# One level of Strassen's algorithm for the two products of a channel mixer

## The chip, the cores and the metric

The kernel runs on one core of one Trainium2 chip. The metric is the device time of one execution in microseconds (us). A core has a matrix engine (TensorE, here PE, with its weight loads as PEld), three others for elementwise work (VectorE or DVE, ScalarE or ACT, GpSimd or POOL) and a queue that issues transfers (SyncE or SP). Each works through its own list of instructions in order and waits on the others by semaphores. SBUF and PSUM are the on-chip memories: PE writes its products into banks of PSUM.

## The reference

One decoder layer over 1024 tokens of width 1024: two kinds of attention, merged and projected, and then the channel mixer with 4096 inner features, which is what the change touches:

```
x = x + rmsnorm(merged @ w_out, post_norm_mix)
h2 = rmsnorm(x, pre_norm_mlp)
y = square(relu(h2 @ w_up)) @ w_down
x = x + rmsnorm(y, post_norm_mlp)
```

All in float32.

## The kernel before

Every float32 matrix is held as a sum of two rounded parts, hi and lo (`hilo`, L80: a copy to hi on ACT, a subtraction for lo on DVE or another engine), and every product is made of three passes in `mm3` (L85): hi by hi, hi by lo, lo by hi. One pass over 128 rows and 512 columns is one matmul instruction, called a product or a pass below.

Ahead of the channel mixer, `mix_front` and `mix_back` (L914, L937) go over 8 tiles of 128 tokens: w_out, norm, residual, second norm, transposes on PE, and the split of the transposed activation into h2 (two halves of 512 tokens, each hi and lo, 8 blocks of 128 features).

The mixer follows in 16 groups of two chunks of 128 inner features. `up(g)` loads two chunks of w_up (512 KB each), splits them (`wchunk`, L132), makes 2 x 2 x 8 x 3 products into PSUM (`big`), and then relu and square on ACT and the split of the result (`uh`, `ul`) on DVE. It stays in SBUF. `down(g)` takes these as stationary operands with the two chunks of w_down (`dh`, `dl`), goes over 8 token tiles and two column halves, and adds each bank `D` to the sum `yac` in SBUF on DVE (L1040). In the program `up(g + 1)` stands before `down(g)`, and a scheduler orders each engine's list. Loads go through two buffers `raw`. The last group also makes the final norm, tile by tile, and stores the output. The last tile is cut into pieces of 512, 256 and 256 columns.

## Time and profile before

| | us |
|---|---|
| median of 3 runs (1430.97 to 1434.01) | 1433.59 |
| span of the profiled execution | 1434.7 |
| PE busy in it | 1403.1 (98%) |
| DVE busy | 764.5 (53%) |
| ACT busy | 534.0 (37%) |
| POOL busy | 231.8 (16%) |
| the channel mixer, from its first product to the end | 722.6 to 1434.7 |

The profile is one execution recorded by the hardware. A page sums it up (busy time by engine, the chain of instructions that ended last, groups of instructions, transfers), and views of the trace give the instructions of one engine in order of time, groups of equal instructions, and the busy time of each engine in a stretch. PEclk is the clock that PE was granted, as a share of full speed.

### The profile page before, as it was taken

The numbers are of one execution on the slowest core, as the hardware profiler recorded it, in microseconds if no ns is written. First come the engines' busy times: TensorE is split into PE (matmuls) and PEld (weight loads), VectorE is DVE, ScalarE is ACT, GpSimd is POOL, SyncE is SP. The second block draws the span as 40 slices with busy tenths as digits, with TensorE's granted clock in tenths as the row PEclk, the third lists the DMA queues.
The fourth block names the chain that finished last, engine by engine and source line by source line (L and its number), as shares of the span: only waits on it lengthen the run. The fifth ranks groups of instructions, "written<-read, shape, count | busy, mean of one in ns | idle before, by whom it ended". The sixth has DMA issues, their size and how long they took to land.

```text
span 1434.7 us, 17738 instructions
## 1 busy us (share of the span) xinstructions
PE 1403.1 (98%) x6650; PEld 1155.2 (81%) x6650; DVE 764.5 (53%) x1339; ACT 534.0 (37%) x977; POOL 231.8 (16%) x316
## 2 busy tenths in 40 slices
...
GB/s 316 118 93 127 112 120 92 124 113 87 100 98 93 130 176 245 220 228 89 94 98 88 59 31 43 45 59 60 56 31 32 59 59 59 30 45 44 59 1 205
DMA packets 64183, 141.24 MB, mean 98 GB/s; under 512 B 8417, under 2 KB 22625, under 8 KB 64097
## 3 DMA queue, kind: packets, MB, share of 16 engines
...
## 4 chain that ended last, share of the span: by engine, by line
PE 84%; DMA 6%; DVE 5%; ACT 2%; issue 2%; POOL 1%; SPq 1%; POOLq 0%; DVEq 0%; ACTq 0%
PE big L87 12%; PE big L88 12%; PE big L89 12%; PE D L88 8%; PE D L87 8%; PE D L89 8%; PE F L87 4%; PE F L88 4%; PE F L89 4%; DMA raw<-w_o 2%; PE T L784 2%; PE big L758 1%; PE big L755 1%; PE big L759 1%; DVE wlo L83 1%
## 5 line engine op out<-in xcount | busy, mean ns | idle before, releaser
L89 PE MATMUL big<-h,wlo 128*128 128x512 f32 x748 | 295.1, 395 | 7.5 <-DVE wlo L83 7.5
L87 PE MATMUL big<-h,whi 128*128 128x512 f32 x748 | 294.2, 395 | 1.5 <-DVE sg L907 0.8
L88 PE MATMUL big<-l,whi 128*128 128x512 f32 x748 | 294.4, 394 | 0.0
L82 ACT CAST whi<-raw 128x1024 fp32r<-128x1024 f32 (+1 forms) x89 | 91.8, 1033 | 441.0 <-PE big L88 382.6
L1040 DVE TENSOR_TENSOR yac<-D,yac 128x512 f32<-128x512 f32 (+1 forms) x225 | 154.0, 686 | 143.3 <-PE D L89 142.6
L88 PE MATMUL D<-dl,uh 128*128 128x512 f32 (+1 forms) x516 | 200.1, 388 | 0.0
L87 PE MATMUL D<-dh,uh 128*128 128x512 f32 (+1 forms) x516 | 200.0, 388 | 0.0
L89 PE MATMUL D<-dh,ul 128*128 128x512 f32 (+1 forms) x516 | 199.5, 387 | 0.0
L89 PEld LDWEIGHTS big<-h,wlo 128*128 128x128 f32 x748 | 141.1, 189 | 43.0 <-DVE wlo L83 12.1
L83 DVE TENSOR_TENSOR wlo<-raw,whi 128x1024 fp32r<-128x1024 f32 (+1 forms) x73 | 94.5, 1296 | 143.1 <-ACT whi L82 138.3
L87 PEld LDWEIGHTS big<-h,whi 128*128 128x128 f32 x748 | 140.9, 189 | 32.8 <-ACT h L82 1.2
L88 PEld LDWEIGHTS big<-l,whi 128*128 128x128 f32 x748 | 141.1, 189 | 30.9
L103 POOL TENSOR_SCALAR s<-s 128x1 f32<-128x1 f32 x24 | 4.9, 205 | 772.9 <-DVE s L1046 692.1
L87 PEld LDWEIGHTS D<-dh,uh 128*128 128x128 f32 x516 | 96.9, 188 | 20.2
L88 PEld LDWEIGHTS D<-dl,uh 128*128 128x128 f32 x516 | 96.9, 188 | 20.0
L89 PEld LDWEIGHTS D<-dh,ul 128*128 128x128 f32 x516 | 96.9, 188 | 19.9
L88 PE MATMUL F<-l,whi 128*128 128x512 f32 x260 | 103.4, 398 | 3.2 <-DVE l L83 3.2
L87 PE MATMUL F<-h,whi 128*128 128x512 f32 x260 | 104.7, 403 | 0.6 <-ACT h L82 0.5
L89 PE MATMUL F<-h,wlo 128*128 128x512 f32 x260 | 103.2, 397 | 0.0
L83 DVE TENSOR_TENSOR dl<-raw,dh 128x1024 fp32r<-128x1024 f32 x32 | 39.1, 1225 | 94.8 <-ACT dh L82 94.8
L82 ACT CAST dh<-raw 128x1024 fp32r<-128x1024 f32 x32 | 33.5, 1050 | 132.3 <-DMA raw<-w_down 111.1
L768 POOL TENSOR_SCALAR e<-e,bsm 128x128 f32<-128x128 f32 (+3 forms) x64 | 49.1, 771 | 138.3 <-DVE bsm L767 99.6
...
## 6 DMA issues: line engine op xcount, KB each, us to landing
raw<-w_in SPq DMA_DIRECT2D x42, 512.0 KB, 3.8
raw<-w_up SPq DMA_DIRECT2D x32, 512.0 KB, 3.8
raw<-w_down SPq DMA_DIRECT2D x32, 512.0 KB, 3.6
x<-x SPq DMA_DIRECT2D x24, 512.0 KB, 3.6
gate<-tmp SPq DMA_DIRECT2D x32, 256.0 KB, 2.0
sg<-gate SPq DMA_DIRECT2D x32, 256.0 KB, 4.0
raw<-w_o SPq DMA_DIRECT2D x15, 512.0 KB, 4.7
xT<-xT SPq DMA_DIRECT2D x16, 256.0 KB, 5.8
```

The lines of the kernel that those rows point to most:

```text
L82: nc.scalar.copy(out=hi, in_=src)
L83: (eng or nc.vector).tensor_tensor(out=lo, in0=src, in1=hi.bitcast(F32), op=ALU.subtract)
L87: nc.tensor.matmul(out, lhsT=lh, rhs=rh, start=first, stop=False)
L88: nc.tensor.matmul(out, lhsT=lh, rhs=rl, start=False, stop=False)
L89: nc.tensor.matmul(out, lhsT=ll, rhs=rh, start=False, stop=last)
L103: nc.gpsimd.tensor_scalar(out=out, in0=ss, scalar1=1.0 / dim, scalar2=EPS, op0=ALU.mult, op1=ALU.add)
L755: nc.tensor.matmul(o, lhsT=qh, rhs=kh[:, kc], start=True, stop=False)
L758: nc.tensor.matmul(o, lhsT=qh, rhs=kl[:, kc], start=False, stop=False)
L759: nc.tensor.matmul(o, lhsT=ql, rhs=kh[:, kc], start=False, stop=True)
L768: nc.gpsimd.tensor_scalar(out=e[:, :nk], in0=e[:, :nk], scalar1=sm[:, 3:4], scalar2=1.0, op0=ALU.mult, op1=ALU.mult)
L784: nc.tensor.transpose(pt[:, c0:c0 + P], es2[qi][:, kb * P:(kb + 1) * P], ident)
L1040: nc.vector.tensor_tensor(out=y[:, nn], in0=ps, in1=y[:, nn], op=ALU.add)
```

## The change

The mixer's two matrix products are each cut into 2 x 2 blocks, and the eight block products are replaced by seven, between sums of blocks (Winograd's form of Strassen's algorithm). There are now two stages with the result in DRAM between them.

- `mix_back` writes the transposed activation H unsplit (odd k on ACT, even k on DVE). `split_b1` splits the first half of the tokens during tile 4. The first w_up pair is loaded during the last tile, and its products p1 and p2 (banks `F` and `O`) stand around the last tile's transposes.
- After the last tile, a loop over k makes four sums of blocks of H (b11, b12, b22, b21 in place, two on DVE and two on POOL) and splits five operands `B1[p]` for p = 5, 6, 7, 4, 3, with the subtraction on DVE, for p = 7 on POOL.
- The up stage goes over 16 pairs j of w_up chunks. `up_w` makes four sums of the weights on POOL (`s`) and five splits (`oh`, `ol`, six buffers each); `raw1` and `raw2` share the two buffers `raw`. `up_head` and `up_tail` of neighbouring pairs are interleaved. Products accumulate in banks a, b and c, copies are kept on ACT (`snap`) and added on DVE (`summed`). Relu and square are on ACT. Four further sums on POOL combine the squared results for the next stage (`v`), and all seven parts go to DRAM (`UC`, 256 KB each).
- The down stage goes over 8 groups. `down_ops` loads four chunks of w_down (`r1`, `r2`) and the seven parts (`ur`, two buffers), makes four sums on POOL (`t1`, `t2`, b12 and `t2` again), and splits both operands, four of the fourteen subtractions on POOL and ten on DVE. `down_step` makes a product for one of four token tiles and adds the bank to `yac`, 28 such additions a group. One bank is carried on from one product to the next, and opened anew at products 1, 5 and 2.
- The cut of the last tile is gone, and the final multiplication by `gpo` is on POOL.

The core of the diff:

```diff
-                hi, lo = act_k(h2[ti // 4], 4 * a + k)
+                dst = H[ti // 4][:, 4 * a + k, c]
                 gk = g_mlp[:, 4 * a + k:4 * a + k + 1]
                 src = pt[:, k * P:(k + 1) * P]
-                nc.scalar.activation(out=hi[:, c], in_=src, func=AF.Copy, scale=gk)
-                nc.vector.scalar_tensor_tensor(out=lo[:, c], in0=src, scalar=gk, in1=hi.bitcast(F32)[:, c],
-                                               op0=ALU.mult, op1=ALU.subtract)
+                if k % 2:
+                    nc.scalar.activation(out=dst, in_=src, func=AF.Copy, scale=gk)
+                else:
+                    nc.vector.tensor_scalar(out=dst, in0=src, scalar1=gk, scalar2=None, op0=ALU.mult)
...
+    H = [tl(act["0"], [P, KD, 512], F32, tag, 1) for tag in "hl"]
+    UC = {p: [tc.dram_tile([P, 2, 512], F32, name=f"uc_{p}_{g}") for g in range(NGRP)] for p in range(1, 8)}
...
+    def up_w1(j):
+        raw = tl(wst, [P, 1024], F32, "raw", 2)
+        nc.sync.dma_start(out=raw, in_=t["w_up"][2 * j])
+        hi, lo = tl(wst, [P, 1024], F32R, "whi", 2), tl(wst, [P, 1024], F32R, "wlo", 2)
+        hilo(hi, lo, raw)
+        ws = {1: (hi[:, :512], lo[:, :512]), 2: (hi[:, 512:], lo[:, 512:])}
+        return raw, ws
...
+    def split_b1():
+        hi, lo = act_set("2")
+        for k in range(0, KD, 2):
+            hilo(hi[:, k:k + 2, :], lo[:, k:k + 2, :], H[0][:, k:k + 2, :])
+        B1[1] = hi[:, 0:4, :], lo[:, 0:4, :]
+        B1[2] = hi[:, 4:8, :], lo[:, 4:8, :]
...
+        if ti == NT - 1:
+            early_up = up_w1(0)
         if len(pend) > 1:
             mix_back(*pend.pop(0))
+        if ti == 4:
+            split_b1()
+    banks[0] = dict(a=fbank(), b=tl(pss, [P, 512], F32, "O", 1))
+    up_mm(banks[0]["a"], early_up[1][1], B1[1], True)
+    up_mm(banks[0]["b"], early_up[1][2], B1[2], True)
     mix_back(*pend.pop())
...
+    for k in range(4):
+        b11, b21, b12, b22 = H[0][:, k, :], H[0][:, 4 + k, :], H[1][:, k, :], H[1][:, 4 + k, :]
+        of = {p: (B1[p][0][:, k, :], B1[p][1][:, k, :]) for p in (5, 6, 7, 4, 3)}
+        nc.vector.tensor_tensor(out=b11, in0=b12, in1=b11, op=sub)
+        hilo_on(nc.vector, *of[5], b11)
+        nc.gpsimd.tensor_tensor(out=b12, in0=b22, in1=b12, op=sub)
+        hilo_on(nc.vector, *of[3], b22)
+        nc.vector.tensor_tensor(out=b22, in0=b22, in1=b11, op=sub)
+        hilo_on(nc.vector, *of[6], b22)
+        hilo_on(nc.gpsimd, *of[7], b12)
+        nc.gpsimd.tensor_tensor(out=b21, in0=b21, in1=b22, op=sub)
+        hilo_on(nc.vector, *of[4], b21)
...
+    def up_w(j):
+        raw1, ws = early_up if j == 0 else up_w1(j)
+        raw2 = tl(wst, [P, 1024], F32, "raw", 2)
+        nc.sync.dma_start(out=raw2, in_=t["w_up"][2 * j + 1])
+        a11, a12, a21, a22 = raw1[:, :512], raw1[:, 512:], raw2[:, :512], raw2[:, 512:]
+        s = {p: tl(uw, [P, 512], F32, "s", 4) for p in (5, 6, 7, 3)}
+        def split(p, x):
+            hi, lo = tl(uw, [P, 512], F32R, "oh", 6), tl(uw, [P, 512], F32R, "ol", 6)
+            hilo(hi, lo, x)
+            ws[p] = hi, lo
+        nc.gpsimd.tensor_tensor(out=s[5], in0=a21, in1=a22, op=add)
+        split(5, s[5])
+        nc.gpsimd.tensor_tensor(out=s[6], in0=s[5], in1=a11, op=sub)
+        split(6, s[6])
+        nc.gpsimd.tensor_tensor(out=s[7], in0=a11, in1=a21, op=sub)
+        split(7, s[7])
+        split(4, a22)
+        nc.gpsimd.tensor_tensor(out=s[3], in0=a12, in1=s[6], op=sub)
+        split(3, s[3])
+        return ws
+    def snap(ps):
+        x = slot(2)
+        nc.scalar.copy(out=x, in_=ps)
+        return x
+    def relu2(x, src):
+        nc.scalar.activation(out=x, in_=src, func=AF.Relu)
+        nc.scalar.activation(out=x, in_=x, func=AF.Square)
+    def store_u(j, p, x):
+        nc.sync.dma_start(out=UC[p][j // 2][:, j % 2, :], in_=x)
+    def summed(j, p, x, ps, s):
+        nc.vector.tensor_tensor(out=x, in0=ps, in1=s, op=add)
+        relu2(x, x)
+        store_u(j, p, x)
+    def up_head(j, w, after=None):
+        b = banks.setdefault(j, {})
+        if j:
+            b["a"] = tl(ps4, [P, 512], F32, "a", 2)
+            up_mm(b["a"], w[1], B1[1], True)
+        s1 = snap(b["a"])
+        if after:
+            after()
+        b["c"] = tl(ps4, [P, 512], F32, "c", 2)
+        up_mm(b["c"], w[5], B1[5], True)
+        up_mm(b["a"], w[6], B1[6], False)
+        b["s2"] = snap(b["a"])
+        if j:
+            b["b"] = tl(pss, [P, 512], F32, "T", 2)
+            up_mm(b["b"], w[2], B1[2], True)
+        u = b["u"] = {p: slot(0) for p in (1, 2, 5, 4)}
+        summed(j, 1, u[1], b["b"], s1)
+        up_mm(b["a"], w[7], B1[7], False)
+        s3 = snap(b["a"])
+        summed(j, 4, u[4], b["c"], s3)
+    def up_tail(j, w):
+        b = banks.pop(j)
+        u = b["u"]
+        up_mm(b["a"], w[4], B1[4], False)
+        relu2(u[2], b["a"])
+        store_u(j, 2, u[2])
+        up_mm(b["c"], w[3], B1[3], False)
+        x = u[5]
+        nc.vector.tensor_tensor(out=x, in0=b["c"], in1=b["s2"], op=add)
+        relu2(x, x)
+        v = {p: slot(1) for p in (5, 6, 7, 3)}
+        for p, a0, a1, op in ((5, x, u[4], add), (6, v[5], u[1], sub), (7, u[1], x, sub), (3, u[2], v[6], sub)):
+            nc.gpsimd.tensor_tensor(out=v[p], in0=a0, in1=a1, op=op)
+            store_u(j, p, v[p])
+    w = up_w(0)
+    up_head(0, w)
+    for j in range(1, NP):
+        w_next = up_w(j)
+        up_head(j, w_next, lambda: up_tail(j - 1, w))
+        w = w_next
+    up_tail(NP - 1, w)
...
-    us = up(0)
-    for g in range(NGR - 2):
-        cur = us
-        us = up(g + 1)
-        down(cur, down_w(g), first=g == 0)
-    us = us + up(NGR - 1)
-    down(us, down_w(NGR - 2) + down_w(NGR - 1), last=True)
+    ORDER = (1, 6, 7, 4, 5, 3, 2)
+    def dslots(z):
+        return tl(p5, [P, 2, 512], F32R, z + "h", 7), tl(p5, [P, 2, 512], F32R, z + "l", 7)
+    def down_ops(g):
+        r1, r2 = (tl(p5, [P, 2, 1024], F32, "r1", 2 if f == 0 else 2) for f in range(2))
+        for f, r in enumerate((r1, r2)):
+            for q in range(2):
+                nc.sync.dma_start(out=r[:, q, :], in_=t["w_down"][4 * g + 2 * q + f])
+        b11, b12, b21, b22 = r1[:, :, :512], r1[:, :, 512:], r2[:, :, :512], r2[:, :, 512:]
+        t1, t2 = tl(p5, [P, 2, 512], F32, "t1", 1), tl(p5, [P, 2, 512], F32, "t2", 1)
+        ops = {}
+        def one(p, src):
+            x = tl(p5, [P, 2, 512], F32, "ur", 2)
+            nc.sync.dma_start(out=x, in_=UC[p][g])
+            u, w = dslots("u"), dslots("w")
+            hilo_on(nc.gpsimd if p in (7, 5, 3) else nc.vector, *u, x)
+            hilo_on(nc.gpsimd if p == 2 else nc.vector, *w, src)
+            ops[p] = u, w
+        one(1, b11)
+        nc.gpsimd.tensor_tensor(out=t1, in0=b12, in1=b11, op=sub)
+        nc.gpsimd.tensor_tensor(out=t2, in0=b22, in1=t1, op=sub)
+        one(6, t2)
+        nc.gpsimd.tensor_tensor(out=b12, in0=b22, in1=b12, op=sub)
+        one(7, b12)
+        nc.gpsimd.tensor_tensor(out=t2, in0=b21, in1=t2, op=sub)
+        one(4, t2)
+        one(5, t1)
+        one(3, b22)
+        one(2, b21)
+        return ops
...
+    OPENS = (1, 5, 2)
+    def down_step(g, p, op, i, ps):
+        down_mm(ps, op, i, p in OPENS)
+        r, n = DEST[p]
+        y = yac[:, i + r, 512 * n:512 * n + 512]
+        if g == 0 and p in (1, 6, 7, 4):
+            nc.scalar.copy(out=y, in_=ps)
+        else:
+            nc.vector.tensor_tensor(out=y, in0=ps, in1=y, op=add)
+    def dbank():
+        return tl(psd, [P, 512], F32, "D", 8)
...
+    for g in range(NGRP):
+        ops = down_ops(g)
+        if g < NGRP - 1:
+            for p in ORDER:
+                if p in OPENS:
+                    bank = [dbank() for _ in range(4)]
+                for i in range(4):
+                    down_step(g, p, ops[p], i, bank[i])
+            continue
+        for i in range(4):
+            low, high = finish_in(i), finish_in(4 + i)
+            for p in ORDER:
+                if p in OPENS:
+                    ps = dbank()
+                down_step(g, p, ops[p], i, ps)
+                if p == 4:
+                    finish_a(4 + i, *high, 0)
+                elif p == 5:
+                    finish_a(4 + i, *high, 1)
+                    finish_b(4 + i, *high)
+                elif p == 3:
+                    finish_a(i, *low, 1)
+                elif p == 2:
+                    finish_a(i, *low, 0)
+                    finish_b(i, *low)
```

The scheduler's order at the places that change most. First DVE at the entry into the mixer, before: the last splits of the last tile (`l` out of PSUM bank `T`), then weights and activations of the mixer.

```order
L949 SCALAR_TENSOR_TENSOR l_1320_6919<-T_1346_7289,g_mlp_6_80,h_1319_6918 128x128
L83 TENSOR_TENSOR wlo_1365_7442<-raw_1363_7439,whi_1364_7441 128x1024
L1005 CAST uh_1358_7428<-r_1357_7425 128x1024
L1006 TENSOR_TENSOR ul_1359_7429<-r_1357_7425,uh_1358_7428 128x1024
L83 TENSOR_TENSOR wlo_1369_7449<-raw_1367_7446,whi_1368_7448 128x1024
L83 TENSOR_TENSOR dl_1379_7566<-raw_1377_7563,dh_1378_7565 128x1024
```

After, DVE's list there (`h_1295` and `l_1296` are the two halves of H): L1031 and L1022 make sums of H and the lo parts of the operands 6 and 4, L84 those of weights, with `ol_1389` the one for product 5 of the second pair:

```order
L1022 TENSOR_TENSOR l6_1355_7347<-l_1296_6587,h6_1354_7346 128x512
L84 TENSOR_TENSOR ol_1378_7442<-s_1368_7420,oh_1377_7441 128x512
L1022 TENSOR_TENSOR l6_1355_7347<-l_1296_6587,h6_1354_7346 128x512
L1031 TENSOR_TENSOR l_1296_6587<-l_1296_6587,h_1295_6586 128x512
L84 TENSOR_TENSOR wlo_1382_7496<-raw_1380_7493,whi_1381_7495 128x1024
L1022 TENSOR_TENSOR l6_1355_7347<-l_1296_6587,h6_1354_7346 128x512
L1022 TENSOR_TENSOR l4_1359_7351<-h_1295_6586,h4_1358_7350 128x512 x2
L1022 TENSOR_TENSOR l6_1355_7347<-l_1296_6587,h6_1354_7346 128x512
L1022 TENSOR_TENSOR l4_1359_7351<-h_1295_6586,h4_1358_7350 128x512
L84 TENSOR_TENSOR ol_1389_7507<-s_1384_7501,oh_1388_7506 128x512
```

and on POOL, sums of H (L1029, L1034), operand 7, and the first weight sum of the second pair:

```order
L1029 TENSOR_TENSOR l_1296_6587<-l_1296_6587 128x512
L1034 TENSOR_TENSOR h_1295_6586<-h_1295_6586,l_1296_6587 128x512 x2
L1022 TENSOR_TENSOR l7_1357_7349<-l_1296_6587,h7_1356_7348 128x512 x2
L1034 TENSOR_TENSOR h_1295_6586<-h_1295_6586,l_1296_6587 128x512
L1022 TENSOR_TENSOR l7_1357_7349<-l_1296_6587,h7_1356_7348 128x512
L1059 TENSOR_TENSOR s_1384_7501<-raw_1383_7499 128x512
```

What was a row of splits out of PSUM and of weights is now a longer row with inputs in SBUF on two engines. On SP's queue before, the loads of both weights alternate all through the mixer, each waiting for a DMA queue and for DVE to release its buffer:

```order
L134 DMA raw_1579_9023<-w_up 128x1024 [waits DMAHW0_49,DVE_49]
L134 DMA raw_1583_9030<-w_up 128x1024 [waits DMAHW6_49,DVE_49]
L1014 DMA raw_1593_9147<-w_down 128x1024 [waits DMAHW1_49,DVE_49]
L1014 DMA raw_1596_9153<-w_down 128x1024 [waits DMAHW3_49,DVE_49]
L134 DMA raw_1615_9287<-w_up 128x1024 [waits DMAHW4_49,DVE_49]
```

After, the last stores of the up stage, and behind them the first loads of the down stage:

```order
L1080 DMA uc_6_7_6635<-l_1363_7414 128x512 [waits DMAHW2_49,Pool_49]
L1080 DMA uc_3_7_6611<-l_1363_7414 128x512 [waits DMAHW3_49,Pool_49]
L1142 DMA gpo_1695_9764<-g_po 128x1024 [waits DMAHW4_49,DVE_49]
L1153 DMA r1_1697_9767<-w_down 128x1024 [waits DMAHW3_49,DMAHW2_49,DMAHW5_49,DMAHW1_49,DMAHW6_49,DMAHW0_49,DMAHW7_49,DVE_49,Activation_49]
L1153 DMA r1_1697_9767<-w_down 128x1024
L1153 DMA r1_1698_9768<-w_down 128x1024 x2
L1160 DMA ur_1701_9775<-uc_1_0_6588 128x1024 [waits PE_49]
```

The load of w_down into `r1` now waits on all DMA queues, and on DVE and ACT. DVE's list within the down work, before (L1040 adds a bank to `yac`; the others prepare operands):

```order
L1040 TENSOR_TENSOR yac_1348_7314<-D_1671_9687,yac_1348_7314 128x512
L83 TENSOR_TENSOR wlo_1693_9825<-raw_1691_9822,whi_1692_9824 128x1024
L1040 TENSOR_TENSOR yac_1348_7314<-D_1672_9695,yac_1348_7314 128x512
L1005 CAST uh_1663_9671<-r_1662_9668 128x1024
L1040 TENSOR_TENSOR yac_1348_7314<-D_1673_9703,yac_1348_7314 128x512
L1006 TENSOR_TENSOR ul_1664_9672<-r_1662_9668,uh_1663_9671 128x1024
L1040 TENSOR_TENSOR yac_1348_7314<-D_1674_9711,yac_1348_7314 128x512
```

and within a group of the down stage after (L1196 adds a bank, L1022 makes lo parts):

```order
L1022 TENSOR_TENSOR ul_1805_10358<-ur_1803_10355,uh_1804_10357 128x1024
L1022 TENSOR_TENSOR wl_1807_10360<-r1_1799_10347,wh_1806_10359 128x1024
L1196 TENSOR_TENSOR yac_1696_9766<-D_1787_10139,yac_1696_9766 128x512
L1196 TENSOR_TENSOR yac_1696_9766<-D_1788_10140,yac_1696_9766 128x512
L1196 TENSOR_TENSOR yac_1696_9766<-D_1789_10141,yac_1696_9766 128x512
L1196 TENSOR_TENSOR yac_1696_9766<-D_1790_10142,yac_1696_9766 128x512
L1022 TENSOR_TENSOR ul_1810_10370<-ur_1808_10367,uh_1809_10369 128x1024
L1022 TENSOR_TENSOR wl_1812_10372<-t2_1802_10354,wh_1811_10371 128x1024
```

The additions now stand in fours between pairs of splits.

## Rows read from the trace of the kernel before

**Rows 1.** The page's shares of busy time, and its chain that ended last.

```profile
PE 1403.1 (98%) x6650; PEld 1155.2 (81%) x6650; DVE 764.5 (53%) x1339; ACT 534.0 (37%) x977; POOL 231.8 (16%) x316
...
PE 84%; DMA 6%; DVE 5%; ACT 2%; issue 2%; POOL 1%; SPq 1%; POOLq 0%; DVEq 0%; ACTq 0%
```

**Rows 2.** Windows: busy us (instructions) of PE, PEld, DVE, ACT, POOL; clock, DMA, GB/s.

```profile
715.00:1415.00 700.00, 699.98 (x3071) 574.86 (x3070) 302.50 (x394) 153.34 (x190) 7.31 (x16) 1.00 0.18 55
```

**Rows 3.** POOL's timeline: start, us, line, operation, idle time before it and its releaser.

```profile
578.63 2.20 POOL L908 TENSOR_TENSOR mx<-sg 128x512 f32<-128x512 f32 x1 [7.80 <-DVE sg L907]
...
595.35 1.30 POOL L908 TENSOR_TENSOR mx<-sg 128x512 f32<-128x512 f32 x1 [5.24 <-DVE sg L907]
```

**Rows 4.** DVE's timeline in the same place.

```profile
578.47 1.22 DVE L83 TENSOR_TENSOR wlo<-raw,whi 128x1024 fp32r<-128x1024 f32 x1
579.60 1.78 DVE L83 TENSOR_TENSOR l<-omc,h 128x512 fp32r<-128x512 f32 x1
581.52 0.69 DVE L83 TENSOR_TENSOR l<-mx,h 128x512 fp32r<-128x512 f32 x1
582.13 1.22 DVE L907 TENSOR_TENSOR sg<-big,sg 128x1024 f32<-128x1024 f32 x1
```

**Rows 5.** DVE's timeline where its input lies in PSUM.

```profile
274.72 0.69 DVE L83 TENSOR_TENSOR h<-big,h 128x512 fp32r<-128x512 f32 x1 [1.33 <-ACT h L82]
```

**Rows 6.** POOL's timeline at that moment.

```profile
273.64 2.40 POOL L83 TENSOR_TENSOR wlo<-raw,whi 128x1024 fp32r<-128x1024 f32 x1 [3.21 <-ACT whi L82]
```

**Rows 7.** PE's timeline where the last tile ahead of the mixer ends.

```profile
722.37 0.39 PE L89 MATMUL big<-woh,l 128*128 128x512 f32 x1
722.60 0.39 PE L87 MATMUL big<-h,whi 128*128 128x512 f32 x1
...
723.29 1.03 PE L943 MATMUL T<-ident,y 128*128 128x128 f32 x8
```

**Rows 8.** DVE's timeline there.

```profile
730.01 0.75 DVE L934 TENSOR_SCALAR y<-x,s 128x1024 f32<-128x1024 f32 x1
...
735.41 3.15 DVE L949 SCALAR_TENSOR_TENSOR l<-T,g_mlp,h 128x128 fp32r<-128x128 f32 x8 [4.40 <-ACT h L948]
```

**Rows 9.** Groups of instructions on ACT by shape: count | busy us, mean ns | idle before.

```profile
L82 ACT CAST dh<-raw 128x1024 fp32r<-128x1024 f32 x32 | 33.5, 1050 | 132.3 <-DMA raw<-w_down 111.1 <-PE D L89 21.1
...
L82 ACT CAST bth<-T 128x512 fp32r<-128x512 f32 x48 | 27.4, 590 | 2.3 <-PE T L784 2.0
...
L1042 ACT ACTIVATE r<-yac 128x512 f32<-128x512 f32 x15 | 9.5, 631 | 29.6 <-DVE yac L1040 29.6
```

**Rows 10.** The page's DMA issues: count, KB each, median us to landing.

```profile
raw<-w_up SPq DMA_DIRECT2D x32, 512.0 KB, 3.8
raw<-w_down SPq DMA_DIRECT2D x32, 512.0 KB, 3.6
...
gate<-tmp SPq DMA_DIRECT2D x32, 256.0 KB, 2.0
```

**Rows 11.** SP's timeline (its DMA queue): start, us, the issue.

```profile
728.27 0.43 SPq L982 DMA_DIRECT2D gpo<-g_po  x1
```

**Rows 12.** Windows at the kernel's start and end, columns as in rows 2.

```profile
8.00:9.00 1.00, 0.00 (x0) 0.00 (x0) 1.00 (x1) 0.82 (x2) 0.88 (x1) 1.00 1.01 414
10.00:11.00 1.00, 1.00 (x4) 0.78 (x4) 1.00 (x3) 0.89 (x1) 0.00 (x0) 0.66 1.06 408
11.00:12.00 1.00, 1.00 (x4) 0.72 (x4) 0.60 (x2) 1.00 (x3) 0.77 (x1) 0.50 1.08 418
...
13.00:14.00 1.00, 1.00 (x4) 0.49 (x2) 1.00 (x1) 0.62 (x2) 0.66 (x1) 0.64 1.02 408
1425.00:1430.00 5.00, 2.21 (x19) 2.01 (x17) 3.58 (x9) 1.74 (x6) 0.97 (x3) 1.00 0.30 114
```

**Rows 13.** Groups on DVE by shape, columns as in rows 9.

```profile
L1040 DVE TENSOR_TENSOR yac<-D,yac 128x512 f32<-128x512 f32 x223 | 153.2, 689 | 143.3 <-PE D L89 142.6
...
L83 DVE TENSOR_TENSOR dl<-raw,dh 128x1024 fp32r<-128x1024 f32 x32 | 39.1, 1225 | 94.8 <-ACT dh L82 94.8
```

**Rows 14.** Groups on POOL by shape.

```profile
L83 POOL TENSOR_TENSOR wlo<-raw,whi 128x1024 fp32r<-128x1024 f32 x16 | 38.4, 2401 | 57.2 <-ACT whi L82 57.2
```

**Rows 15.** PE's timeline near the kernel's start.

```profile
9.48 0.50 PE L88 MATMUL big<-l,ewh 128*128 128x512 f32 x1 [1.81 <-DVE l L209]
```

**Rows 16.** DVE's timeline at the kernel's end.

```profile
1430.28 1.54 DVE L1049 SCALAR_TENSOR_TENSOR yac<-yac,s,x 128x512 f32<-128x512 f32 x3 [1.02 <-POOL s L104]
```

More of the change, by code (lines that the diff above doesn't have):

```diff
@@ L31 @@
 SCALE_B = 96 ** -0.5
-GROUP = 2
+NP = NFF // 2
+NGRP = NP // 2
 WARM = 14
```

133 lines of the change are left out of this document (56 added, 77 removed).

## The prediction

> **What bounds the kernel now.** Read the shares of busy time and the chain of waits first [rows 1]: TensorE (PE) works in 98% of the span, VectorE (DVE) in 53%, GpSimd (POOL) in 16%, and 84% of the chain that ends last is PE. Then the stretch of the channel mixer alone [rows 2]: from 715 to 1415 us PE is never idle, so 3071 products take 700 us, **0.2279 us each**, at a granted clock of 1.00, while DVE is busy 43%, POOL 1% and the DMA engines 18%. Nothing but PE is late there. A change that takes products away must win their time, if the engines that now feed PE can keep it fed. So the question is not the saving but where PE will wait. The durations come from the one profiled execution, whose span is 1434.7 us; the median of the runs shown is 1433.59, 1.1 less, and I take 1.1 off at the end.
>
> **The saving.** Products of 128x512 in the mixer: before, 32 chunks x 2 halves x 8 blocks x 3 passes = 1536 up and as many down. After, 16 pairs x 7 products x 4 blocks x 3 = 1344 up, and 8 groups x 7 x 4 x 2 x 3 = 1344 down. So 384 go: 384 x 0.2279 = **-87.5 us**.
>
> **A fact about two engines.** What the change adds on DVE and POOL are additions and splits, mostly with both inputs in SBUF. POOL takes 1.30 us for such an operation on 512 columns when DVE does nothing of that kind, but 2.20 when it starts 0.16 us after one on DVE [rows 3]. That one, `wlo`, runs from 578.47 for 1.22 us; DVE's next one then takes 1.78 in place of some 0.69, and ends 0.55 us after POOL's [rows 4]. So POOL waited for DVE's operation to end and DVE for POOL's: **they alternate and don't overlap**. Operations of DVE that read PSUM are not touched: `h<-big,h` took 0.69 in the middle of a 2.40 us POOL operation [rows 5, 6]. Before, POOL had hardly any work beside the mixer; after, it has 8 operations in each pair and in each group.
>
> [...]
>
> **A. Entry into the mixer.** Before, the last tile of the mixer ahead gets its norm while up products run, from 722.60 on [rows 7]: y is ready at 730.76 and DVE's last split of it ends at 738.56 [rows 8], with no wait of PE. After, PE has only the two products p1 and p2 of the first pair (24 x 0.2279 = 5.5) and 8 transposes (1.03 [rows 7]), and is out of work at 729.1. Then the sums of the activation must be made. H is ready from 730.8 + 1.0 + 0.6 = 732.4. PE goes on in order: c of pair 0 (12 products), p1 and p2 of pair 1 (24), c of pair 1, and the last needs `ol_1389`. By the order DVE has 29 operations of 512 with two SBUF inputs up to that one, and one of 1024; POOL has 16, of which 3 need no H. Alternating: DVE 29 x 0.62 (the pitch of such operations in a row, as 0.69 long ones start 0.61 apart [rows 4]) = 18.0, + 1.2, + POOL 13 x 1.30 = 16.9, + about 4 for handing over between ACT, DVE and POOL: 732.4 + 40 = 772. PE without a wait would be there at 722.6 + 60 x 0.2279 + 1.0 = 737.3: 35 late. The loads of pairs 2 and 3 use the same two raw buffers and start behind this, +3: I take **+38**. If nothing excluded anything, DVE alone needs 19.2 + 1.5: 753, **+16**. Upper bound 45, with 8 more of handing over.
>
> **U. The up stage, per pair.** PE 84 x 0.2279 = 19.1. None of the others has as much: POOL 8 x 1.30 = 10.4; DVE 5 splits of 512, one of 1024 (1.22) and three sums out of PSUM, 7; ACT 11 [rows 9]. But one chain goes round once a pair: the c product ends, a split frees the second raw buffer (0.6 ACT + 0.69 DVE), it is loaded (3.8 [rows 10]), POOL makes four sums (5.2), which frees the first buffer, loaded again (3.8), cast (1.05), and 14 products (3.2) lead to the next end of c: 18.4, + six handovers of about 0.15, + DVE's operations in POOL's way, 0 to 2.8. I take 20.6, 1.5 more than PE: 13 pairs in the steady state, **+20** (0 to 45). The stores of U parts that stand between on SP's queue (six 256 KB ones a pair, 2.0 us each [rows 10], issued in some 0.4 [rows 11]) don't keep the loads back unless POOL is late.
>
> **B. From up to down.** `r1`, the first load of w_down, waits on the queue for the last store of up. After the last product: sum 0.7, relu and square 1.2, four POOL sums 5.2, issue and store 2.4 = 9.5. [...] Then the first group goes as fast as its loads and POOL's 8 operations; +3. **+23** (17 to 30).
>
> **D. The down stage, per group.** PE 168 x 0.2279 = 38.3. DVE: 28 evictions x 0.689 (all out of PSUM) + 10 splits x 1.22 = 31.5 [rows 13]. POOL: 4 splits of 1024 and 4 sums of 1024, 8 x 2.40 = 19.2 [rows 14]. Both kinds together: 12.2 + 19.2 = 31.4 of 38.3. So DVE has 6.8 us a group to wait for POOL before it bounds. By the order four evictions stand between two splits in most places; they fill the time of a POOL operation, and I count waits of 5 to 7: about even. PE needs an eviction done before it adds the next product to the bank, 4.1 us later, which takes up single waits. **+7** in all (1 in each of 7 groups; 0 to 87, if each POOL operation delays DVE in full: 31.5 + 19.2 = 50.7).
>
> **Tail and clock.** Before, the last product ends at 1427.2 (2.21 us into the window from 1425), and DVE's last at 1431.8 [rows 12, 16]. After, the last block has one chain of seven products with its sums: two gaps of about 1, and POOL's multiplication by `gpo` (1.30 for 0.69) is ahead of the last norm: **+4**. [...] At the entry and before down: **+3**.
>
> **Sum.** 1434.7 - 87.5 + 38 + 20 + 23 + 7 + 4 + 3 = 1442.2, less 1.1: **1441**. The forecast with its own range: 1415 to 1465.
>
> **Rivals.** (1) *POOL's work hides.* DVE and POOL find each other's gaps, since DVE idles half the time. Then A 16, U 3 (19.3 a pair), B 21, D 0, tail 4, clock 3: 47; 1434.7 - 87.5 + 47 - 1.1 = **1393**. For it: POOL's and DVE's mean load is far below PE's in U and D. Against it: at A both have a full queue, and the price of meeting is 0.9 us on POOL and 1.1 on DVE [rows 3, 4]. (2) *DVE bounds down* (slower). Each split waits behind POOL, and with the splits the evictions queued behind them, so that banks come free late. It decides from 6.8 us of waits per group; with 12, half-way to the upper bound's 19.2 plus what POOL does in evictions, a group is 43.5, 5.2 more than PE, 7 x 5.2 = 37 in place of 7: **1471**. For it: POOL's 2.40 is longer than three evictions (2.07). (3) *Part by part right, but shifted by chains I don't see*, such as the six buffers `oh` and `ol` or SP's in-order stores: inside the forecast's range.
>
> **How the numbers follow.** Forecast 0.47, rival 1 0.33, rival 2 0.20. A measurement of this kernel tells about 0.2% (2.9 us) from no change. Faster: rival 1, and the forecast's part under 1430.7 (U and D at their lower ends), 0.13: 0.46. Same: 0.07, out of the forecast. Slower: the rest of it, 0.27, + 0.20 = 0.47. Range 1380 to 1485: it leaves out rival 1 with a boundary shorter than 17 (0.07) and rival 2 with waits of over 14 (0.09).
>
> **What would show it.** PE busy about 1316 (87.5 less) whatever comes. Right: PE idle 30 to 45 us in the first 60 us of the mixer, with POOL operations of 512 over 1.3 and DVE's splits over 0.69; an idle stretch of about 20 before the first product into D; pairs of 20 to 21 us; groups of 38 to 40. Wrong: pairs at 19.1 and an entry under 20 (rival 1), groups over 41 that wait for evictions (rival 2), or an entry chain that is held by ACT or by loads and not by DVE and POOL.

## The result, and the profile after

The changed kernel takes **1473.03 us** (median, 1469.95 to 1477.02) where the one before takes 1433.69 (1430.97 to 1434.01): 1.0277 times as long, with an interval of 1.0257 to 1.0297. It is 39 us slower. The forecast was 1441, so the sign of the likeliest case was right, though slower and faster had nearly the same chance there (0.47 and 0.46), and the size was far off. The rival in which DVE bounds the down stage gave 1471, close to the measured time, but by a way that did not come (see D below): that nearness is chance. The profiled execution has a span of 1475.2 us, 40.5 more than the one before.

The page's shares and its chain that ended last, of the kernel after, to be held against [rows 1]:

```profile
PE 1348.9 (91%) x6254; PEld 1098.1 (74%) x6254; DVE 897.1 (61%) x1396; ACT 682.7 (46%) x1223; POOL 631.6 (43%) x536
...
PE 42%; DMA 17%; POOL 14%; DVE 11%; issue 10%; ACT 4%; SPq 1%; POOLq 0%; DVEq 0%; ACTq 0%
```

PE's share of the chain fell from 84% to 42%. DMA, POOL, DVE and issue took its place. Where PE waits, and for whom, stands in PE's waits over the whole run (us in total, times, longest):

```profile
PE T L88 <- ACT whi L83: 23.0, 10, 4.4
PE D L88 <- ACT uh L1021: 20.3, 1, 20.3
PE a L90 <- DVE wlo L84: 8.4, 1, 8.4
```

The largest is not at a border between stages: ten waits for a cast of w_up (`whi`), up to 4.4 us each, one of them (0.8 us) at the entry and the other nine in the up stage. Two windows show what that costs, one in the up and one in the down stage (columns as in [rows 2]):

```profile
800.00:900.00 100.00, 91.56 (x378) 73.49 (x378) 38.70 (x42) 46.09 (x79) 54.00 (x39) 0.95 0.40 137
1200.00:1300.00 100.00, 98.97 (x434) 81.26 (x435) 88.06 (x105) 36.58 (x37) 57.90 (x22) 1.00 0.43 143
```

At 0.2279 us each [rows 2], 100 us have room for 439 products. The down stage makes 434, the up stage 378.

**A balance by stages.** From PE's timeline I take the length of each stage, less 0.2279 for each product in it; the rest is its loss. "Entry" is the first 157 products of the mixer (until 794 us), "up" the other 1187 products of the up stage, "gap" the time from the last product of up to the first of down, "group 0" the first 168 products of down, "middle" six groups, "last" the eighth, "end" what follows PE's last product. The letters are those of the prediction.

| loss, us | after | forecast |
|---|---|---|
| entry (A) | 36.9, of it idle 25.7, low clock 5.6 | 38 |
| up (U) | 40.7, of it idle 25.0, low clock 12.0 | 20 |
| gap and group 0 (B) | 20.4 + 10.8 = 31.2 | 20 + 3 = 23 |
| middle (D) | 5.8 | 7 |
| last and end, less before's 12.0 | 6.4 + 20.3 - 12.0 = 14.7 | 4 |
| clock | in the rows above | 3 |
| sum | 129.3 | 95 |

The 12.0 is what the mixer had before: 712.1 us for 3072 products, which are 700.1; 7.5 of it came after the last product. 129.3 less the 87.5 saved, and less 1.2 because the first up product comes earlier (721.37 for 722.60), is +40.6. The spans differ by 40.5. As a loss is whatever a stage takes beyond 0.2279 for each product, the losses must add up to that difference: the balance tells where the time lies, and the experiments tell why.

### The profile page after: what moved, and what is told of

It reads as the page before. It is cut to its first block, busy times and chain, and to the rows that moved or that the text cites. A ratio compares the mean times of both kernels' runs of the same rounds, so it can differ in the third digit from the quotient of the medians.

```text
span 1475.2 us, 18186 instructions
## 1 busy us (share of the span) xinstructions
PE 1348.9 (91%) x6254; PEld 1098.1 (74%) x6254; DVE 897.1 (61%) x1396; ACT 682.7 (46%) x1223; POOL 631.6 (43%) x536
## 4 chain that ended last, share of the span: by engine, by line
PE 42%; DMA 17%; POOL 14%; DVE 11%; issue 10%; ACT 4%; SPq 1%; POOLq 0%; DVEq 0%; ACTq 0%
DMA raw<-w_up 6%; PE big L90 4%; PE big L89 4%; PE big L88 4%; PE F L88 4%; PE F L89 4%; PE F L90 4%; DMA r<-w_down 4%; DMA ur<-uc 2%; DMA raw<-w_o 2%; POOL ul L1022 2%; POOL l L1121 2%; PE T L785 2%; DVE wl L1022 2%; POOL wl L1022 2%
## 5 line engine op out<-in xcount | busy, mean ns | idle before, releaser
L88 PE MATMUL D<-wh,uh 128*128 128x512 f32 x448 | 177.5, 400 | 34.1 <-ACT uh L1021 20.3
L89 PE MATMUL D<-wl,uh 128*128 128x512 f32 x448 | 177.3, 396 | 0.0
L90 PE MATMUL D<-wh,ul 128*128 128x512 f32 x448 | 173.6, 394 | 0.0
L1196 DVE TENSOR_TENSOR yac<-D,yac 128x512 f32<-128x512 f32 x208 | 131.1, 679 | 11.9 <-PE D L90 11.7
L88 PEld LDWEIGHTS D<-wh,uh 128*128 128x128 f32 x448 | 85.9, 192 | 57.6 <-ACT uh L1021 20.7
L84 DVE TENSOR_TENSOR wlo<-raw,whi 128x1024 fp32r<-128x1024 f32 (+1 forms) x57 | 72.8, 1277 | 83.2 <-ACT whi L83 78.0
L84 DVE TENSOR_TENSOR ol<-s,oh 128x512 fp32r<-128x512 f32 x64 | 62.1, 971 | 79.7 <-ACT oh L83 79.0
L90 PE MATMUL big<-h,wlo 128*128 128x512 f32 x236 | 94.8, 402 | 5.3 <-DVE wlo L84 5.3
L89 PEld LDWEIGHTS D<-wl,uh 128*128 128x128 f32 x448 | 86.0, 192 | 17.7
L90 PEld LDWEIGHTS D<-wh,ul 128*128 128x128 f32 x448 | 85.4, 191 | 18.2
L88 PE MATMUL big<-h,whi 128*128 128x512 f32 x236 | 94.5, 402 | 0.6 <-ACT whi L83 0.6
L89 PE MATMUL big<-l,whi 128*128 128x512 f32 x236 | 94.2, 399 | 0.0
L1022 POOL TENSOR_TENSOR ul<-ur,uh 128x1024 fp32r<-128x1024 f32 x24 | 64.9, 2705 | 52.7 <-ACT uh L1021 45.5
```

What stands on the lines that cost most here:

```text
L84: (eng or nc.vector).tensor_tensor(out=lo, in0=src, in1=hi.bitcast(F32), op=ALU.subtract)
L88: nc.tensor.matmul(out, lhsT=lh, rhs=rh, start=first, stop=False, skip_group_check=chain)
L89: nc.tensor.matmul(out, lhsT=lh, rhs=rl, start=False, stop=False, skip_group_check=chain)
L90: nc.tensor.matmul(out, lhsT=ll, rhs=rh, start=False, stop=last, skip_group_check=chain)
L1022: eng.tensor_tensor(out=lo, in0=src, in1=hi.bitcast(F32), op=sub)
L1196: nc.vector.tensor_tensor(out=y, in0=ps, in1=y, op=add)
```

## The experiments

Effects of single edits below 8 us are not sure where the up stage still pauses: the times of such a kernel lie up to 11.5 us apart, and the kernel before, run again beside the experiments, took 1433.0 to 1435.9 in the median. There the stages of the profiled run decide. Losses by stage, in us:

| kernel | entry | up | gap | group 0 | middle | last + end |
|---|---|---|---|---|---|---|
| after | 36.9 | 40.7 | 20.4 | 10.8 | 5.8 | 26.7 |
| third raw buffer | 36.6 | 6.8 | 20.7 | 11.2 | 2.2 | 26.8 |
| early loads for down | 36.5 | 41.2 | 4.1 | 15.0 | 3.8 | 27.0 |
| sums on DVE | 29.4 | 34.9 | 21.0 | 10.8 | 4.3 | 26.5 |
| x2 all loaded early | 36.5 | 36.2 | 20.7 | 10.7 | 5.3 | 23.8 |
| the same, gpo on DVE | 36.3 | 37.4 | 20.2 | 10.8 | 4.0 | 22.1 |
| the same, tiles by pairs | 36.5 | 35.9 | 20.1 | 10.6 | 4.6 | 23.9 |
| combined | 30.5 | 6.6 | 4.2 | 14.6 | 3.9 | 23.2 |
| combined, early sums | 23.3 | 7.7 | 4.2 | 14.7 | 5.1 | 22.4 |
| the same, by pairs, gpo on DVE | 24.5 | 6.2 | 4.1 | 14.5 | 5.0 | 17.0 |
| the same, by pairs, gpo on POOL | 25.2 | 5.7 | 4.1 | 14.7 | 3.8 | 23.4 |

### The up stage: a third buffer for w_up

Before the experiment, one turn of the chain as the kernel after has it. SP's queue:

```profile
974.56 3.26 SPq L1080 DMA_DIRECT2D uc<-l  x3
977.92 0.38 SPq L1050 DMA_DIRECT2D raw<-w_up  x1
...
988.33 0.33 SPq L979 DMA_DIRECT2D raw<-w_up  x1
```

DVE's, POOL's and ACT's timelines, each in its own fence:

```profile
975.09 1.24 DVE L84 TENSOR_TENSOR ol<-raw,oh 128x512 fp32r<-128x512 f32 x1 [2.12 <-ACT oh L83]
```

```profile
973.25 2.54 POOL L1121 TENSOR_TENSOR l<-h 128x512 f32<-128x512 f32 x2 [7.23 <-ACT h L1077]
975.75 1.73 POOL L1121 TENSOR_TENSOR l<-l,h 128x512 f32<-128x512 f32 x1
...
982.23 1.29 POOL L1059 TENSOR_TENSOR s<-raw 128x512 f32<-128x512 f32 x1 [3.38 <-DMA raw<-w_up]
983.60 1.29 POOL L1061 TENSOR_TENSOR s<-s,raw 128x512 f32<-128x512 f32 x1
984.86 1.74 POOL L1063 TENSOR_TENSOR s<-raw,raw 128x512 f32<-128x512 f32 x1
986.56 1.74 POOL L1066 TENSOR_TENSOR s<-raw,s 128x512 f32<-128x512 f32 x1
```

```profile
970.06 1.05 ACT L83 CAST whi<-raw 128x1024 fp32r<-128x1024 f32 x1 [5.43 <-DMA raw<-w_up]
```

And PE's, behind a cast of 1.05 us on ACT:

```profile
993.62 0.79 PE L88 MATMUL T<-h,whi 128*128 128x512 f32 x1 [2.94 <-ACT whi L83]
...
996.77 0.45 PE L90 MATMUL c<-h,ol 128*128 128x512 f32 x1
```

From the end of one c product (974.7) to the end of the next (998.45) this turn takes 23.75 us: 1.6 until the split ends at 976.33; 1.6 until SP has issued three stores, the last of which waited for POOL's third sum to end at 977.48, and reaches the load; 4.3 for the load; 6.1 for four sums; 4.2 for the next load; 1.1 for the cast; 4.8 for 14 products. Those would be 3.2, but seven of them are 0.42 to 0.6 apart, until 996.77: the clock was lower after the pause (0.52 granted from 994 to 997). The turn is longer than the mean, 22.0.

POOL was late here because ACT works in order: the input of the pair's last relu was ready at 966.43, but relu and square stood behind the cast of `whi`, which waited 5.43 us for its load, and POOL's sums and their stores followed only from 973.25. In eleven of the sixteen pairs that relu started 2 to 6 us after its input was ready.

```diff
-        raw2 = tl(wst, [P, 1024], F32, "raw", 2)
+        raw2 = tl(uw, [P, 1024], F32, "rawb", 1)
```

> The changed kernel, with a third buffer for the weights of the up stage: the second load of a pair has one of its own, the first ones have the two old ones. Theory: the pairs take 22.0 us and not 19.1, since a chain goes round once a pair: c product, split, load of the second raw, four sums on POOL, load of the first raw, cast, 14 products. With the third buffer the first load doesn't wait for the pair's sums, the chain is cut, and PE is never late in the steady state: pairs of 19.2 to 19.6, with a granted clock of 1.00: 14 x 2.4 = 30 to 38 less, about 1440. Rival: POOL and DVE in each other's way set the pace (POOL's sums take 1.74 and not 1.29 there), or the stores ahead of the loads on SP's queue: then the pairs stay above 21, and the time above 1462.

Measured: 1439.0 (1435.9 to 1441.29), 1.0028 times before [1.0013, 1.0044]; 34 us less than the kernel after, in the expected -30 to -38. The loss of up goes from 40.7 to 6.8, and no other stage moves by more than 4. PE's waits from 795 to 1070 us in this kernel, and then the same window as above:

```profile
PE a L88 <- ACT l L1072: 2.6, 2, 1.9
```

```profile
800.00:900.00 100.00, 100.00 (x438) 81.96 (x437) 48.41 (x47) 50.59 (x86) 64.39 (x44) 1.00 0.48 153
```

The wait for `whi` is gone, and 438 products fit into 100 us. POOL and DVE do more work in it than in the kernel after, so neither of them was the bound. The loss was the ring of two buffers, with a load on both sides of POOL's sums. How much of it each link of the ring makes, this run does not tell, for it cuts them all at once.

### Whether the stores on SP hold the loads back

In the turn above the load is issued 1.6 us after its buffer came free, behind three stores. Here the stores of a pair's four POOL sums are issued after the next pair's loads in the program's text; the sums of one pair are overwritten before their store, so that part of the result is not computed.

```diff
-            store_u(j, p, v[p])
+            held.append((j, p, v[p]))
...
         w_next = up_w(j)
+        flush()
```

> The changed kernel, with the stores of a pair's four sums v issued in the program behind the next pair's load of the second raw, not ahead of it; buffers as in the changed kernel. Theory: the chain of one pair (22.0 us) holds a wait of some 1.5 us of the second raw's load behind three stores on SP's queue (974.6 to 977.9 in the trace); without it the pairs are 20.5 to 21, and the clock falls less often: 14 x 1 to 1.5 = 14 to 21 less, about 1456. Rival: the loads are then held by the splits and by POOL's sums, and v by the stores that free its places: 0 to 5 less, about 1470.

Measured: 1475.95 (1473.37 to 1478.06). It tells nothing, for the scheduler put the stores back where they were. SP's queue in this kernel:

```profile
968.87 3.26 SPq L1080 DMA_DIRECT2D uc<-l  x3
972.22 0.38 SPq L1050 DMA_DIRECT2D raw<-w_up  x1
```

What the stores' place alone costs was not measured. The trace of the kernel after tells how often it comes: of the second loads of the thirteen pairs from 795 to 1070 us, six left 1.6 us after their buffer came free, each behind a store that waited for POOL, and seven left at once. That is 9.5 us of waiting in the whole stage, beside its loss of 40.7.

### From up to down: the first loads issued before the last pair's end

```diff
+    pre_r = down_r(0)
+    pre_u = {p: down_u(0, p) for p in (1, 6)}
     up_tail(NP - 1, w)
```

The buffers for these (r1, r2 and two ur) lie in a pool of their own, opened where h2 of one half is closed, ahead of the last pair's tail. The load of gpo goes behind group 0.

> The changed kernel, with the first group's loads of w_down (r1, r2) and of the parts 1 and 6 issued before the last tail of the up stage, into a pool in the memory of B1[1] and B1[2], and the down stage's other buffers laid so that the first ones come on memory that is free early. Theory: PE's 20.3 us without work before the first product of the down stage are the sums and stores of the last pair (9.5) and then loads and casts (11), because the first load waits for the last stores; the loads move into the up stage. The products then start at most 3 us after the last up product and wait some 4 us for yac, which lies on the ring of the last stores: 12 to 18 less, about 1458. Rival: the first group is held by its POOL operations and by the loads of parts 7, 4, 5 anyway, and the gap moves into the group: 3 to 8 less, about 1467.

Measured: 1460.23 (1458.7 to 1468.24), 12.8 less than after, in the expected 12 to 18. The gap falls from 20.4 to 4.1, so its cause was that r1 and ur came behind the last stores, on SP's queue and for their memory; the edit moves both together. Four of the 16 come back in group 0 (10.8 to 15.0). Of the kernel after, SP and PE at the border:

```profile
1108.84 4.09 SPq L1080 DMA_DIRECT2D uc<-l  x4
1113.03 0.38 SPq L1142 DMA_DIRECT2D gpo<-g_po  x1
1115.01 1.76 SPq L1153 DMA_DIRECT2D r<-w_down  x4
```

```profile
1125.69 0.79 PE L88 MATMUL D<-wh,uh 128*128 128x512 f32 x1 [20.27 <-ACT uh L1021]
...
1138.89 0.79 PE L88 MATMUL D<-wh,uh 128*128 128x512 f32 x1 [5.47 <-ACT yac L1194]
```

The second wait is group 0's. `yac`, a plain copy of PSUM on ACT, is late because ACT works in order, and ahead of it stand casts that wait for POOL:

```profile
1134.47 1.99 ACT L1021 CAST wh<-t 128x1024 fp32r<-128x1024 f32 x2 [1.78 <-POOL t L1172]
1136.37 1.99 ACT L1021 CAST wh<-r 128x1024 fp32r<-128x1024 f32 x2
1138.27 0.57 ACT L1194 COPY yac<-D 128x512 f32<-128x512 f32 x1
```

POOL makes `t` beside a DVE split of 1024, and both take about 3.3 us, 2.40 and 1.22 apart from each other [rows 13, 14]:

```profile
1131.15 3.29 POOL L1172 TENSOR_TENSOR t<-r,t 128x1024 f32<-128x1024 f32 x1 [1.16 <-DVE wl L1022]
```

```profile
1132.13 3.40 DVE L1022 TENSOR_TENSOR wl<-r,wh 128x1024 fp32r<-128x1024 f32 x1
```

### The entry: DVE and POOL at the same work

DVE and then POOL of the kernel after, where the sums of H are made:

```profile
741.07 1.75 DVE L84 TENSOR_TENSOR ol<-s,oh 128x512 fp32r<-128x512 f32 x1
742.74 1.77 DVE L1022 TENSOR_TENSOR l<-l,h 128x512 fp32r<-128x512 f32 x1
744.44 1.74 DVE L1031 TENSOR_TENSOR l<-l,h 128x512 f32<-128x512 f32 x1
```

```profile
740.56 1.71 POOL L1066 TENSOR_TENSOR s<-raw,s 128x512 f32<-128x512 f32 x1
742.23 1.73 POOL L1022 TENSOR_TENSOR l<-l,h 128x512 fp32r<-128x512 f32 x1
743.93 1.71 POOL L1029 TENSOR_TENSOR l<-l 128x512 f32<-128x512 f32 x1
```

Each engine starts one operation every 1.69 us: operations of DVE that start 0.61 apart without POOL here take turns with those of POOL. The edit gives POOL's two sums and its split in the loop over H to DVE, three times in each of four blocks:

```diff
-        nc.gpsimd.tensor_tensor(out=b12, in0=b22, in1=b12, op=sub)
+        nc.vector.tensor_tensor(out=b12, in0=b22, in1=b12, op=sub)
...
-        hilo_on(nc.gpsimd, *of[7], b12)
-        nc.gpsimd.tensor_tensor(out=b21, in0=b21, in1=b22, op=sub)
+        hilo_on(nc.vector, *of[7], b12)
+        nc.vector.tensor_tensor(out=b21, in0=b21, in1=b22, op=sub)
```

> The changed kernel, with all the work on H at the entry (sums and splits in the loop over k) on DVE, none on POOL. Theory: operations of DVE and POOL with two inputs in SBUF don't overlap, so the entry costs the sum of both; POOL's 12 operations at 1.3 us then become 12 at 0.62 on DVE: 12 x 0.67 = 8 us less, less what POOL could do in DVE's gaps: 4 to 8 less, about 1467. Rival: the two engines work side by side, and the entry is as long as DVE's list: 12 x 0.62 = 7 us more, about 1480.

Measured: 1465.93 (1458.47 to 1469.65), 7.1 less; the entry's loss falls from 36.9 to 29.4. That is in the expected 4 to 8. DVE got 12 operations more, and its operations are 0.60 apart there. Its timeline in this kernel, and then POOL's:

```profile
744.13 0.68 DVE L1022 TENSOR_TENSOR l<-l,h 128x512 fp32r<-128x512 f32 x1
744.73 0.68 DVE L1034 TENSOR_TENSOR h<-h,l 128x512 f32<-128x512 f32 x1
```

```profile
745.92 6.56 POOL L1059 TENSOR_TENSOR s<-raw 128x512 f32<-128x512 f32 x1 [15.77 <-DMA raw<-w_up]
```

So turn by turn is not all that can happen: this sum of POOL took 6.56 us for 1.30, while DVE went on with eight operations close behind one another, none of them longer than alone.

### The end: x2, gpo and the order of the tiles

Of the kernel after, PE's last product starts at 1454.70, and DVE goes on for 17 us:

```profile
1468.27 1.41 DVE L1214 SCALAR_TENSOR_TENSOR yac<-yac,s,x 128x512 f32<-128x512 f32 x2 [3.70 <-DMA x<-x]
1470.73 1.42 DVE L1214 SCALAR_TENSOR_TENSOR yac<-yac,s,x 128x512 f32<-128x512 f32 x2 [1.05 <-DMA x<-x]
```

The residual x2 of eight tiles comes through two buffers. The first edit gives each tile its own place, in buffers of w_down that are free by then, and loads all ahead of the last group:

```diff
+        fin = [(finish_in(i), finish_in(4 + i)) for i in range(4)]
...
-            low, high = finish_in(i), finish_in(4 + i)
+            low, high = fin[i]
```

> The changed kernel, with the eight residual tiles x2 of the last group in eight places (two buffers x2, the two r1 buffers and t1 and t2, all free by then) and not in two buffers in turn. Theory: after its last product (1455.1 us in the trace) the changed kernel needs 20 us, because each x2 load waits for the buffer of the tile two before, 4 to 5.6 us a load, and PE itself waits at the end of the last group for additions on DVE that stand behind these. Then the end comes about 8 to 9 us after the last product as in the kernel before, and PE's last waits (3.4 us and the fallen clock, 2.4) go too: 1473 - 11 to -15, about 1460. Rival: the multiplications by gpo on POOL and the norms set the end (POOL is busy in 4.8 of each 5 us from 1440 to 1465): then 1 to 4 less, about 1470.

Measured: 1467.57 (1463.98 to 1470.06), 5.5 less, but last and end together only lose 2.9 (26.7 to 23.8), and the up stage, which the edit doesn't touch, is 4.5 shorter in the profiled run. So the loads were not the main cause; of the expectation's two cases the rival (1 to 4 less) is the nearer. With DVE in POOL's place for the multiplication by gpo, the first edit kept:

```diff
-        nc.gpsimd.tensor_tensor(out=y, in0=y, in1=gpo[:, 512 * n:512 * n + 512], op=ALU.mult)
+        nc.vector.tensor_tensor(out=y, in0=y, in1=gpo[:, 512 * n:512 * n + 512], op=ALU.mult)
```

> The kernel of e1_tail_x2, with the final multiplication by gpo on DVE, as in the kernel before, and not on POOL. In e1 the loads of x2 are early, but 17.9 us remain after the last product, and POOL works through its 16 multiplications from 1430 to 1458.6 without a pause. Theory: the tail had two chains side by side, the loads and POOL's multiplications; with both gone the end comes 8 to 11 us after the last product, and PE's waits in the last group go: 1467.6 - 9 to -13, about 1457. Rival: DVE, which then has 16 x 0.68 = 11 us more work in the last group, bounds it: 2 to 4 less, about 1465.

Measured: 1470.28 (1466.35 to 1477.85): no gain over the first edit, against both cases of the expectation. The end falls from 17.7 to 10.7, and PE's loss in the last group rises from 6.1 to 11.4, as evictions on DVE stand behind the norms (PE's longest wait for one is 3.9 us). The third edit, on the first alone, works the last group off by two tokens' tiles at a time, so that two pairs of norms are due halfway through it:

```diff
-        for i in range(4):
+        for pair in ((0, 1), (2, 3)):
+            bank = {}
...
+                for i in pair:
```

> The kernel of e1_tail_x2 (gpo on POOL as in the changed kernel), with the last group's four token tiles taken in two pairs: all seven products of tiles 0 and 1, then of tiles 2 and 3. In e1 and e5 the scheduler works on tiles 0 to 2 at once, and the norms of all eight output tiles fall into the last 20 us (last group and tail lose 6.1 + 17.9 in e1 and 11.4 + 10.7 in e5: moving gpo from POOL to DVE moved the loss from behind the last product to ahead of it). Theory: it is this crowding that costs; by pairs, half of the norms lie beside products, and the two losses together fall from 24 to some 14 to 17: 1467.6 - 7 to -10, about 1459. Rival: the additions on DVE and the chain of a bank through seven products set it, and pairs give PE fewer banks to change between: the same or up to 5 more, about 1470.

Measured: 1470.98 (1463.13 to 1472.92): no gain either, as the rival had it. PE no longer waits in the last group, and the end grows from 17.7 to 24.1.

### All together

Five edits from above in one kernel: x2 early, gpo on DVE, H's sums on DVE, the third buffer, the early loads.

> The changed kernel with all the edits of e1 to e5 at once: x2 in eight places, gpo on DVE, the work on H at the entry on DVE, the third raw buffer, and the early loads of the down stage. Theory: each took its own loss at its own place, so they add up: 1473.0 - 5.5 (x2) - 10 (gpo) - 7.1 (H on DVE) - 34 (third raw) - 12.8 (early loads) = 1404, faster than the kernel before. Rival: what one gives the next stage takes, and only some 50 us come: 1420 to 1430.

Measured: 1418.43 (1415.73 to 1419.47), 0.9876 times before [0.9854, 0.9899]. The single gains, 5.5, 7.1, 34 and 12.8, are 59.4 in sum, and the kernel gained 54.6. The expected 1404 counted some 10 for gpo, which weren't there; the rival's 1420 to 1430 is the nearer.

Next, the sums of H are made by quarters on DVE as each token tile of the second half gets ready, and w_up of pair 1 is loaded and its p1 and p2 multiplied ahead of the loop over H:

```diff
+        if ti > 4:
+            sums(ti - 5)
...
+    sums(3)
+    banks[1] = dict(a=tl(ps4, [P, 512], F32, "a", 2), b=tl(pss, [P, 512], F32, "T", 2))
+    up_mm(banks[1]["a"], early_up[1][1][1], B1[1], True)
+    up_mm(banks[1]["b"], early_up[1][1][2], B1[2], True)
```

> The kernel of e7_combined, with the sums of H made by quarters of 128 tokens, each as soon as its tile is done, while PE still works on the tiles ahead of the mixer, and with the products p1 and p2 of the second pair moved ahead of the rest. Theory: the entry's loss (29 us in e2) is DVE's work of 36 two-input operations and the weights' splits; 12 of them go away from behind the last tile, and PE gets 24 products (5.5 us) that need none: 10 to 13 less than e7, about 1392. Rival: the sums in the last tiles hold up the norm and the transposes there (DVE is busy in 40% of the last 22 us before the mixer), and the gain is under 5: 1400 or more.

Measured: 1410.76 (1408.14 to 1412.84), 7.7 less, short of the 10 to 13 expected; the entry falls from 30.5 to 23.3. The last two have the order by pairs on top of this, one with the gpo multiplication on DVE, one on POOL:

> The kernel of e8_early_sums (gpo on DVE) with the last group's tiles by pairs as in e9. Theory: its last group and tail lose 12.0 + 10.4; with half of the norms beside products of the second pair 6 to 9 of it go: 1410.8 - 7, about 1403. Rival: DVE has 11 us more work than with gpo on POOL in any order, and nothing changes: 1408 to 1412.

> As e10_combined_pairs_dve, with gpo on POOL as in the changed kernel. Theory: with half of the norms beside products POOL's 16 multiplications have the time that DVE has not, so this is the better place: 1 to 4 less than e10, about 1401. Rival: POOL's multiplications and DVE's final operations, with two inputs in SBUF each, take turns, 1.3 + 0.7, and the last norms come later than with DVE alone: 3 to 6 more than e10.

Measured: **1404.02** (1402.82 to 1405.46) with DVE, 0.9791 times before [0.9771, 0.9811]; 1412.52 (1407.14 to 1413.12) with POOL. The first is as expected and 29 us faster than the kernel before. With these orders the choice of engine is worth 8.5 us, against the expectation that POOL is the better place, and more than its rival's 3 to 6. POOL's and DVE's timelines in the second, and DVE's in the first, where the last norms are made:

```profile
1386.69 6.41 POOL L1228 TENSOR_TENSOR yac<-yac,gpo 128x512 f32<-128x512 f32 x4
```

```profile
1386.89 3.42 DVE L1236 SCALAR_TENSOR_TENSOR yac<-yac,s,x 128x512 f32<-128x512 f32 x2
```

```profile
1392.58 1.88 DVE L1228 TENSOR_TENSOR yac<-yac,gpo 128x512 f32<-128x512 f32 x3
...
1395.12 1.40 DVE L1236 SCALAR_TENSOR_TENSOR yac<-yac,s,r 128x512 f32<-128x512 f32 x2
```

Four multiplications take 6.4 us on POOL, three 1.9 on DVE, and two of DVE's last operations take 3.42 beside POOL's multiplications and 1.40 without. On top of the first edit alone, neither the engine nor the order gained time; the combined kernel with gpo on DVE loses 22.4 in last and end with the old order and 17.0 with the tiles by pairs, and 23.4 by pairs with gpo on POOL.

## Why the prediction was right and wrong

- **The saving** was right: 384 products fewer, and where PE isn't kept waiting they are 0.2279 us apart as before (434 of the 439 that 100 us can hold in the down stage, 438 in the up stage with the third buffer). "PE busy about 1316 whatever comes" was wrong: it is 1348.9. About 27 of the 33 are products at the lower clock, which take longer and count as busy.
- **A, the entry** was right, 36.9 for 38, by the mechanism named: DVE and POOL take turns (one operation of each every 1.69 us), and taking POOL's part away makes it shorter (shown by the sums on DVE). The `ol` of pair 1 that the prediction put at 772 was there for PE at 771.3. Some luck is in the nearness of the sums: 36.9 holds 5.6 at the lower clock, which the prediction had in another term. The rival in which POOL's work hides gave 16, and falls here.
- **U, the up stage** is the step that failed, in its size: the chain was the right one (a third buffer removes it, shown), but its 20.6 us a pair was 22.0 (311.2 us for 1187 products, 84 a pair), and the term 20 was 40.7, inside its own 0 to 45. In the turn shown, 23.75 for 18.4 without handovers, the difference is 0.9 in two loads (4.3 and 4.2 for 3.8), 0.9 in the sums (6.1 for 5.2), 1.6 in 14 products at the lower clock (4.8 for 3.2), 0.3 in the split, and 1.6 behind stores, which the prediction said "don't keep the loads back unless POOL is late": POOL was late, in six of thirteen pairs, and the sum had no price for that. The 0.15 for each of six handovers was an estimate; the one from the cast on ACT to PE's product took 0.05 here (993.57 to 993.62). Since PE's own 19.1 is just below, all that is added to the chain is lost in full: 2.9 us a pair over PE's time in place of 1.5. I had a clock term of 3 for two places, and none for pauses within the up stage; the 12.0 at the lower clock in U alone is more than half of U's miss of 20.7.
- **B, up to down**: the gap is 20.4 for 20, and its cause is shown by the early loads. No run shows the term 20 as it was estimated; in its place the trace after has 7.2 from the end of PE's last product to the end of POOL's last sum (1105.42 to 1112.59), 2.4 until the first load into r1 is issued (1115.01), 9.6 until the cast of ur starts (1124.59) and 1.1 until PE's product. Group 0 is 10.8 for 3, of it 4.5 at the lower clock: the prediction had its loads and POOL's eight operations, but not that ACT's copies out of PSUM queue behind casts that wait for POOL (5.5). That is read from the trace after; no run took it away.
- **D, the down stage** was right, 5.8 for 7. PE meets its evictions in time. The rival that DVE bounds it (12 us of waits a group) did not come: PE waits 4.6 us for DVE's evictions from 1136 to 1420 us, and the evictions, which read PSUM, are as short as before (0.679 us for 0.689 [rows 13]) with POOL at work beside them. Their group (count, then busy us, mean ns, idle before):

```profile
L1196 DVE TENSOR_TENSOR yac<-D,yac 128x512 f32<-128x512 f32 x208 | 131.1, 679 | 11.9 <-PE D L90 11.7
```

- **The tail** was 14.7 for 4. I looked at the last block's own chain, and missed that the norms of the tiles ahead of it are still due as PE ends. x2's two buffers are 2.9 of it at most. In the combined kernel, x2 early, gpo on DVE and the tiles by pairs together leave 17.0 of the 26.7 in last and end, so 9.7 of the 14.7 came from that work of DVE and POOL and its order; the last 5 no run took away.
- **The clock** cost about 27 (entry 5.6, up 12.0, group 0 4.5, middle 2.1, last 2.7; each is the time by which products without an idle gap start more than 0.28 us apart) in place of 3, inside the rows above. No run shows the 3, an estimate for the entry and the place before down; in its place the entry lost 5.6 and group 0, behind the gap, 4.5. It is a measure by the distance of products, and holds some short waits too.

The losses of the 1404 us kernel still add up to 71.4, where before had 12.0: 24.5 at the entry, 18.6 at the border and in group 0, 17.0 in the last group and at the end are the most of it. Whether these can be hidden stays open.
